# Second projection: pairs of column tiles by seven products in place of eight for half of k

## The chip, the core and the metric

The program runs on one core of one Trainium2 chip. The metric is the device time of one execution in microseconds (us); the time before is 2892.36 us, the median of 3 runs (2892.21 to 2892.92).

The engines are named as in the profile: PE is the matrix engine (PEld its weight loads), DVE, ACT and POOL are the vector, scalar and GpSimd engines, and SP issues the DMAs. Each engine executes its own instructions in the order in which they stand; a semaphore wait holds everything behind it on that engine.

## What is computed

Two blocks of a network run over 512 tokens of width 2048. The first is a gated delta rule with cross attention and an output projection. The second, which the change touches, is this (cut to what matters):

```python
u = rmsnorm(h, norm_w[l])
proj = jnp.einsum('bsd,dc->bsc', u, w_in[l])          # 2048 -> 8200 columns
(ml_q, ml_k, ml_v, ml_o, ml_z, ml_i, ml_f,
 hg_q, hg_f, hg_i, hg_g) = jnp.split(proj, split_points, axis=-1)
...
h_a = mlstm_chunkwise(q_a, k_a, v_a, i_pre, f_pre)     # 4 heads
h_a = rmsnorm(h_a, ml_norm_w[l].reshape(ML_HEADS, ML_DV)).reshape(Bn, S, ML_WIDTH)
y_a = jax.nn.sigmoid(ml_o) * h_a * jax.nn.silu(ml_z)
...
h_b = hgrn2_chunkwise(q_b, k_b, logf_b, i_b)           # 8 heads
h_b = rmsnorm(h_b, hg_norm_w[l].reshape(HG_HEADS, HG_DV)).reshape(Bn, S, HG_WIDTH)
y_b = h_b * jax.nn.silu(hg_g)
h = h + jnp.einsum('bsc,cd->bsd', jnp.concatenate([y_a, y_b], axis=-1), w_out[l])
e = jnp.einsum('bsr,rd->bsd', p[l], w_pe[l])
gate = jax.nn.sigmoid(jnp.einsum('bsd,de->bse', rmsnorm(h, pe_norm_w[l]), w_pg[l]))
h = h + gate * e
```

The einsum called proj is the second projection. All arithmetic is to hold the accuracy of float32.

## The kernel before

**Tiles.** Activations lie transposed, 128 features by 512 tokens a tile. A projection is cut into jobs, one for each 128 output columns (class `Job`): the job's PSUM tile `acc` collects 16 k-tiles of 128. Each float32 operand is split into a high part of type float32r and the rest (`hi`, `lo` of a weight, `x2h`, `x2l` of an activation), and each k-tile costs three matmuls of 512 columns: hi by high, hi by rest, lo by high (`_unit`, L364). The second projection is 65 jobs: one narrow one of 64 columns with two matmuls a k-tile, and 64 full ones.

**Weights.** They come in pieces of four k-tiles, 128 x 512 float32, 256 KB: a DMA into a ring `raw` of RAW = 6 buffers, then ACT copies the piece to `hi`, then DVE subtracts (`lo` = `raw` - `hi`), into rings of SPL = 5 buffers (`_pump`, L315). PE may thus find up to five pieces ready.

**Order.** The program is written by a planner, `Driver.run` (L397): it keeps an estimated clock of each engine, runs whatever task is ready by these clocks, and fills PE with the next matmuls of the job list in between. What it writes is a fixed order on each engine. A task's data are SBUF tiles from a pool of NSLOT = 75 slots of 128 x 512 (`slot`, L225); a task that finds none waits. PSUM has eight banks, of which up to `maxacc` hold accumulators of jobs.

**The second projection.** The activations `x2h`, `x2l` (32 slots) are made by `x2_task` (L1312) while the first block's output projection ends. The list J2 (L1913) goes: the narrow gate job, then for each mLSTM head k, q and two v tiles, then for each HGRN2 head f, q and i, then the gates o, z and g. When a job ends, `scaled` (L1335) multiplies its PSUM tile by the norm on DVE (tile `pr`), and the head's own tasks go on from there: `ml_task` (L1420) and `hg_task` (L1592) are chains of small matmuls with DVE and ACT steps between, which the planner sets between the projection's matmuls. Each chain leaves normalized tiles in slots (`f_hs`), the gates multiply them, `split_task` (L1239) splits the product, and the second output projection (`w_out2`) uses it. The jobs of `w_pe` (tile `p_h`, two k-tiles each) come after that one. POOL does little here: a mask on `rowb` in each mLSTM head and a 128 x 4 copy `hcd` in each HGRN2 head.

The names in the rows below: `acc` a job's accumulator, `pg` the level products of an HGRN2 head, `z` their operands, `u` its state, `oh` its output, `tr` a transpose, `ss` a sum over partitions by a matmul with ones whose operand is split into `qh`, `ql`, `Cs` the state of an mLSTM head.

Of the kernel before, what the change touches and what calls it, by code (L numbers as in the profile page):

```python
# [18 lines left out]
T = 512  # L19
# [4 lines left out]
RAW, SPL = 6, 5  # L24
NSLOT = 75
LV, LP = 0.3, 0.3
AHEAD = 1.5
# [37 lines left out]
class Job:  # L65

    def __init__(self, w, x, evac, n=T, prio=5.0, begin=None, c0=0):
        self.w, self.x, self.evac, self.n, self.prio, self.begin = w, x, evac, n, prio, begin
        self.cols = slice(c0, c0 + n)
        self.kt = w.shape[1]  # L70
        self.narrow = w.shape[2] < 128
        self.ps = None
        self.drop = False

# [8 lines left out]
class Driver:  # L83
# [5 lines left out]
    def __init__(self, tc, wp, psp, sp):  # L89
# [8 lines left out]
        self.spl_end = []  # L98
# [6 lines left out]
        self.nslot = 0  # L105
        self.table = None
# [195 lines left out]
    def add(self, *jobs):  # L302

        pcs = {j: [] for j in jobs}
        for c0 in range(0, max(j.kt for j in jobs), KC):
            for j in jobs:
                if c0 >= j.kt:
                    continue
                n = min(KC, j.kt - c0)
                p = len(self.pieces)  # L310
                self.pieces.append((j, c0, n))
                for k in range(c0, c0 + n):
                    self.units.append((j, k, p, k == c0 + n - 1, j is jobs[-1]))

    def _pump(self):  # L315
        while self.i_dma < len(self.pieces):
            r = self.i_dma - RAW
            if r >= 0 and (r >= self.i_spl or self.spl_end[r][1] > self.clk["pe"]):
                break
            j, c0, n = self.pieces[self.i_dma]  # L320
            raw = self.wp.tile([128, KC, 128], F32, tag="raw", bufs=RAW, name="raw")
            self.nc.sync.dma_start(out=raw[:, :n, :j.w.shape[2]], in_=j.w[:, c0:c0 + n])
            self.pieces[self.i_dma] = (j, c0, n, raw, self.land(n * 128 * j.w.shape[2]))
# [3 lines left out]
        while self.i_hi < self.i_dma and self.i_hi < self.i_mm + SPL:  # L327
            j, c0, n, raw, tau = self.pieces[self.i_hi]
            if tau > self.clk["pe"] and self.i_hi > self.i_mm:
                break  # L330
            hi = self.wp.tile([128, KC, 128], F32R, tag="hi", bufs=SPL, name="hi")
            self.tau = tau
            m = j.w.shape[2]
            self.act(hi[:, :n, :m], raw[:, :n, :m], AF.Copy)
            self.pieces[self.i_hi] = (j, c0, n, raw, hi, self.tau)
            self.i_hi += 1
        while self.i_spl < self.i_hi:
            j, c0, n, raw, hi, tau = self.pieces[self.i_spl]
            if tau > max(self.clk["pe"], self.clk["dve"]) and self.i_spl > self.i_mm:
                break  # L340
            self.tau = tau
            if j.narrow:
                lo = None
                self.tt(hi[:, :n, 64:], raw[:, :n, :64], hi[:, :n, :64], SUB)
            else:
                lo = self.wp.tile([128, KC, 128], F32R, tag="lo", bufs=SPL, name="lo")
                self.tt(lo[:, :n], raw[:, :n], hi[:, :n], SUB)
            self.pieces[self.i_spl] = (j, c0, n, hi, lo, self.tau)
            self.spl_end.append((self.i_spl, self.tau))
            self.i_spl += 1  # L350

    def _unit_tau(self):

        j, k, p, _, _ = self.units[self.i_unit]
        if p >= self.i_spl or not j.x.f[k].done:
            return None
        t = max(self.pieces[p][5], j.x.f[k].tau)
# [5 lines left out]

    def _unit(self):  # L364
        j, k, p, last_of_piece, last_job = self.units[self.i_unit]
        self.i_unit += 1
        _, c0, _, hi, lo, _ = self.pieces[p]
# [1721 lines left out]
```

## Time and profile before

| | |
|---|---|
| median of 3 runs | 2892.36 us (2892.21 to 2892.92) |
| the profiled execution | 2891.97 us |
| its span, first to last instruction | 2890.2 us |
| PE busy | 2847.4 us, 99% of the span, 15032 matmuls |
| DVE busy | 1716.1 us, 59% |
| ACT busy | 1389.9 us, 48% |
| POOL busy | 98.0 us, 3% |
| chain that ended last | PE 34% of the span, DVE 1% |
| granted TensorE clock | 0.996 of full speed |

Busy is the union of an engine's instructions. A matmul's recorded duration is longer than its pitch, since matmuls overlap in the array; the pitch, from one start to the next, is what PE spends on it. The second projection runs from 1674.7 us, its first matmul, to about 2505 us, where the matmuls of `w_out2` take over. Its stretch is one row of the table of windows below.

### The profile page before, as it was taken

Reading aid. Unit: us, or ns where it says so; the run is one execution under the profiler, and the core shown is the slowest. Engines: PE = TensorE matmul, PEld = TensorE weight load, DVE = VectorE, ACT = ScalarE, POOL = GpSimd, SP = SyncE. Lnnn points to the kernel's source line nnn. Section 1 sums busy time; section 2 is a strip of 40 time slices with the busy share of each in tenths; the row PEclk is TensorE's granted clock in tenths of the full one; section 3 lists DMA queues with packets and bytes.
Section 4 is the critical chain, followed back from the end, with each engine's and each line's share of the span. In section 5 each row is a group of like instructions: output and inputs, shape, how many; then the busy total and the mean of one; then the engine's idle time right before and its main releaser. Section 6 shows DMA issues by size and latency. Waiting matters only on the chain. (4 is left out here: it accounts for less than half of the span.)

```text
span 2890.2 us, 41231 instructions
## 1 busy us (share of the span) xinstructions
PE 2847.4 (99%) x15032; PEld 2380.3 (82%) x15032; DVE 1716.1 (59%) x3323; ACT 1389.9 (48%) x2664; POOL 98.0 (3%) x198
## 2 busy tenths in 40 slices
PE   8999999999999999999999999999999999999998
PEld 7877888888888888888888878888888888888887
DVE  6746687778788777645333364556556565444446
ACT  6544545555555555444222344445555565333444
POOL 2000100000000000000000000000000000000001
PEclk9999999999999999999999999999999999999999
DMA  7422323233232322354433433322222222333334
GB/s 238 149 81 95 119 88 99 96 99 101 74 104 95 96 95 95 103 179 124 130 119 119 145 111 108 95 76 84 81 77 81 86 82 91 121 121 111 92 97 150
DMA packets 179020, 311.05 MB, mean 108 GB/s; under 512 B 25344, under 2 KB 32128, under 8 KB 178816
## 3 DMA queue, kind: packets, MB, share of 16 engines
q1 hardware_dynamic: 178816, 308.41, 33.7%
q8 instruction: 118, 1.93, 0.3%
q14 instruction: 86, 0.70, 0.1%
HBM read 292.34 MB, written 15.99 MB: 107 GB/s over the span
## 5 line engine op out<-in xcount | busy, mean ns | idle before, releaser
L155 DVE TENSOR_TENSOR lo<-raw,hi 128x512 fp32r<-128x512 f32 (+1 forms) x956 | 644.1, 686 | 615.7 <-ACT hi L141 602.4
L141 ACT ACTIVATE hi<-raw 128x512 fp32r<-128x512 f32 (+1 forms) x964 | 590.6, 621 | 822.0 <-PE acc L208 688.1
L208 PE MATMUL acc<-xh,hi 128*128 128x512 f32 x1424 | 581.8, 409 | 0.6 <-DVE vb L155 0.6
L208 PE MATMUL acc<-xl,hi 128*128 128x512 f32 x1424 | 555.4, 390 | 0.0
L208 PE MATMUL acc<-xh,lo 128*128 128x512 f32 x1408 | 550.9, 391 | 1.1 <-DVE lo L155 1.1
L208 PE MATMUL acc<-x2h,hi 128*128 128x512 f32 x1040 | 415.4, 399 | 0.0
L208 PE MATMUL acc<-x2l,hi 128*128 128x512 f32 x1040 | 405.3, 390 | 0.0
L208 PE MATMUL acc<-x2h,lo 128*128 128x512 f32 x1024 | 399.7, 390 | 0.0
L208 PEld LDWEIGHTS acc<-xh,lo 128*128 128x128 f32 x1408 | 264.3, 188 | 59.7 <-DVE lo L155 1.9
L208 PEld LDWEIGHTS acc<-xh,hi 128*128 128x128 f32 x1424 | 267.9, 188 | 53.0 <-issue 1.7
L208 PEld LDWEIGHTS acc<-xl,hi 128*128 128x128 f32 x1424 | 268.2, 188 | 51.1 <-issue 1.7
L208 PE MATMUL acc<-ph,hi 128*128 128x512 f32 x768 | 298.8, 389 | 0.0
L208 PE MATMUL acc<-pl,hi 128*128 128x512 f32 x768 | 298.8, 389 | 0.0
L208 PE MATMUL acc<-ph,lo 128*128 128x512 f32 x768 | 298.8, 389 | 0.0
L208 PEld LDWEIGHTS acc<-x2h,hi 128*128 128x128 f32 x1040 | 195.6, 188 | 37.3
L208 PEld LDWEIGHTS acc<-x2l,hi 128*128 128x128 f32 x1040 | 195.8, 188 | 37.0
L208 PEld LDWEIGHTS acc<-x2h,lo 128*128 128x128 f32 x1024 | 192.2, 188 | 41.2
L208 PEld LDWEIGHTS acc<-pl,hi 128*128 128x128 f32 x768 | 144.1, 188 | 30.2
L208 PEld LDWEIGHTS acc<-ph,hi 128*128 128x128 f32 x768 | 144.1, 188 | 29.9
L208 PEld LDWEIGHTS acc<-ph,lo 128*128 128x128 f32 x768 | 144.1, 188 | 29.7
L160 DVE SCALAR_TENSOR_TENSOR cv<-acc,c_dn_conv,cv 128x511 f32<-128x511 f32 x144 | 107.4, 747 | 28.1 <-ACT cv L141 24.4
L155 DVE TENSOR_TENSOR Xb<-Xb,Nb 128x16 f32<-128x16 f32 (+30 forms) x372 | 113.9, 306 | 8.9
(324 smaller groups left out, 3676.6 us busy)
## 6 DMA issues: line engine op xcount, KB each, us to landing
raw<-w_qkv SPq DMA_DIRECT2D x192, 256.0 KB, 3.2
raw<-w_out SPq DMA_DIRECT2D x192, 256.0 KB, 2.9
raw<-w_z SPq DMA_DIRECT2D x128, 256.0 KB, 3.1
raw<-w_pg SPq DMA_DIRECT2D x76, 256.0 KB, 3.2
gR<-dgc SPq DMA_DIRECT2D x48, 256.0 KB, 4.1
raw<-w_k SPq DMA_DIRECT2D x32, 256.0 KB, 5.2
raw<-w_v SPq DMA_DIRECT2D x32, 256.0 KB, 3.5
raw<-w_xq SPq DMA_DIRECT2D x32, 256.0 KB, 3.1
```

The lines of the kernel that those rows point to most:

```text
L141: self.nc.scalar.activation(out=out, in_=in_, func=func, **kw)
L155: self._v(eng, 0.07 + n / 960, 0.43 + n / 590).tensor_tensor(out=out, in0=a, in1=b, op=op)
L160: self._v(None, 0.13 + free_size(out) / 960, 0).scalar_tensor_tensor(out=out, in0=a, scalar=s, in1=b, op0=op0, op1=op1)
L208: self.nc.tensor.matmul(out, lhsT=lhsT, rhs=rhs, start=start, stop=stop, is_transpose=True if tr else None)
```

## The change

For 29 pairs of jobs (58 of the 64 full ones), the first 8 of the 16 k-tiles are computed in another way. Call B11 and B12 the four first k-tiles of the pair's two column tiles, B21 and B22 the next four, and cut the 512 tokens into halves a and b. Eight products of one block of weights with one half of the tokens become seven, of sums and differences (the Winograd form of Strassen's scheme); each is 4 k-tiles by three matmuls of 256 columns. The other 8 k-tiles stay as they were. The narrow job, four first full jobs and two last ones stay single.

Around it:

- Four differences of weights a pair (`wt`, and one in place in `raw`) are made on POOL, and the four products that use them get their hi and lo parts from POOL too (`tp`, a cast and a subtraction, ring of TB = 3). The other pieces still go by ACT and DVE: 7 a pair in place of 8.
- Sums and differences of activations (`s2h`, `s2l`, 16 slots) are made once, on POOL, and split on ACT and DVE (`x2_sums`).
- Two products collect in two extra PSUM tiles a pair; ACT copies them out (`z0`, `z1`), DVE combines them by four additions of 256 columns, and `scaled` has an addition more for each job.
- With 57 of 73 slots held by activations, sums and weights, the heads' results are written to DRAM (`hgs`) and read back when a gate needs them; the jobs of HGRN2 heads and gates alternate.
- RAW is 8 in place of 6, NSLOT 73 in place of 75; six of the `w_pe` jobs are set ahead of `w_out2`.

```diff
-RAW, SPL = 6, 5
-NSLOT = 75
+RAW, SPL = 8, 5
+NSLOT = 73
+TB = 3
...
+    def add_pair(self, pr):
...
+        u = [(j, c) for c in range(2 * KC, j0.kt, KC) for j in (j0, j1)]
+        usual(*u[0])
+        b11, b12 = load(j0, 0), load(j1, 0)
+        b12.made = False
+        usual(*u[1])
+        b22, b21 = load(j1, KC), load(j0, KC)
+        diff(t1, b12, b11)
+        for q, l in ((0, b11), (5, t1)):
+            product(q, l)
+        diff(t2, b22, t1)
+        diff(b12, b22, b12)
+        for v in u[2:-1]:
+            usual(*v)
+        for q, l in ((3, b22), (6, t2), (7, b12)):
+            product(q, l)
+        diff(t4, b21, t2)
+        usual(*u[-1])
+        for q, l in ((2, b21), (4, t4)):
+            product(q, l)
...
+    def _top(self, op, pe):
...
+            if self.i_tp >= self.i_tm + TB:
+                return False
...
+            self.cp(op.hi, l.raw, eng=pool)
+            self.tt(op.lo, l.raw, op.hi, SUB, eng=pool)
...
+        self.tt(dst.raw, x.raw, y.raw, SUB, eng=pool)
...
+    def _products(self, u):
...
+        return {0: (pr.x.f[k], a, "p", a), 2: (pr.x.f[k + KC], a, 0, a), 3: (pr.comb[k][1], b, 1, a),
+                4: (pr.x.f[k + KC], b, 0, b), 5: (pr.comb[k][0], a, "q", a), 6: (pr.comb[k][0], b, "p", b),
+                7: (pr.comb[k][1], a, "q", b)}[q]
...
+        for n, (w, x) in enumerate(((pc.hi, xh), (pc.hi, xl), (pc.lo, xh))):
+            self.tau = 0.0
+            self.mm(ps[:, oc], w[:, k], x[:, c], start=first and n == 0,
+                    stop=end and n == 2 and q not in (2, 3))
...
+    def _sums(self, pr):
...
+        self.act(z0, pr.acc["p"], AF.Copy)
+        self.act(z1, pr.acc["q"], AF.Copy)
+        self.free_bank(2)
+        yield
+        for o, x, y in ((z0[:, b], z0[:, a], z0[:, b]), (z1[:, a], z1[:, a], z0[:, b]),
+                        (z0[:, b], z0[:, b], z1[:, b]), (z1[:, b], z1[:, b], z1[:, a])):
+            self.tt(o, x, y, ADD)
...
+    def x2_sums():
...
+                tt(t, hi, lo, ADD, eng=pool)
...
+            for o, x, y, op in ((s[:, a], u[:, b], v[:, b], ADD), (s[:, b], s[:, a], u[:, a], SUB),
+                                (t[:, a], u[:, a], u[:, b], SUB), (t[:, b], v[:, a], s[:, b], SUB)):
+                tt(o, x, y, op, eng=pool)
...
     def scaled(job):
...
+        t = yield from need(job.z)
+        yield
+        tt(t, t, job.ps, ADD)
         d.acc_done()
+        tt(t, t, r, MUL)
         return t
...
-        give(f_hs[2 * MLH + h], r)
+        if h >= HGH - 2:
+            give(f_hs[2 * MLH + h], r)
+            return
+        yield
+        d.dma(hgs_[2 * MLH + h], r)
+        free(r)
+        give(f_hm[2 * MLH + h])
...
+    seq = mls + hgs[:2]
+    hgs = hgs[2:]
+    for i in range(max(len(hgs), len(gts))):
+        seq += hgs[i:i + 1] + gts[i:i + 1]
+    seq += [tuple(gl[i:i + 2]) for i in range(0, HGH - 2, 2)]
+    for i, (j0, j1) in enumerate(seq):
+        d.add_pair(Pair(j0, j1, X2, f_s2, drop=(i == len(seq) - 1)))
```

What stands on PE in a job of the projection before, the first of four k-tiles with a transpose of a head between:

```order
L208 MATMUL acc_17355<-x2h_13754,hi_17264 128x512
L208 MATMUL acc_17355<-x2l_13755,hi_17264 128x512
L208 MATMUL acc_17355<-x2h_13754,lo_17266 128x512
L208 MATMUL tr_17365<-ident_87,mcv_17030 128x128 x4
L208 MATMUL acc_17355<-x2h_13912,hi_17264 128x512
L208 MATMUL acc_17355<-x2l_13913,hi_17264 128x512
```

And now on PE in the first pair, where product 0 ends and product 5 begins:

```order
L249 MATMUL acc_16631<-x2h_15787,hi_16516 128x256
L249 MATMUL acc_16631<-x2l_15788,hi_16516 128x256
L249 MATMUL acc_16631<-x2h_15787,lo_16518 128x256
L249 MATMUL acc_16652<-s2h_15846,tp_16375 128x256
L249 MATMUL acc_16652<-s2l_15847,tp_16375 128x256
L249 MATMUL acc_16652<-s2h_15846,tp_16376 128x256
```

Over the program 1392 matmuls of 512 columns are gone from PE and 2436 of 256 columns have come; the weights of product 5 are POOL's `tp`.

On POOL, all that stood from the last head of the first block to the end before:

```order
L180 MEMSET XT 128x512 x2
L180 MEMSET XA 128x256
L185 AFFINE_SELECT rowb<-rowb 128x512 x4
L175 COPY hcd<-z 128x4 x8
L155 TENSOR_TENSOR out<-h1r,gt 128x256 x10
```

And now on POOL one pair of the 29 (`wt` and `raw` differences of weights, `tp` their parts):

```order
L196 TENSOR_TENSOR wt_16373<-raw_18492,raw_18421 128x512
L216 CAST tp_16422<-wt_16373 128x512
L196 TENSOR_TENSOR tp_16423<-wt_16373,tp_16422 128x512
L196 TENSOR_TENSOR wt_16402<-raw_18509,wt_16373 128x512
L196 TENSOR_TENSOR raw_18492<-raw_18509,raw_18492 128x512
L216 CAST tp_16375<-wt_16402 128x512
L196 TENSOR_TENSOR tp_16376<-wt_16402,tp_16375 128x512
L216 CAST tp_16418<-raw_18492 128x512
L196 TENSOR_TENSOR tp_16419<-raw_18492,tp_16418 128x512
L196 TENSOR_TENSOR wt_16460<-raw_18589,wt_16402 128x512
L216 CAST tp_16422<-wt_16460 128x512
L196 TENSOR_TENSOR tp_16423<-wt_16460,tp_16422 128x512
```

Eight two-input subtractions and four casts a pair are new on POOL; `rowb` and `hcd` now stand between them.

On DVE, around the end of a job in an HGRN2 head before:

```order
L155 TENSOR_TENSOR lo_19247<-raw_19092,hi_19245 128x512
L155 TENSOR_TENSOR pr_19253<-acc_19127,ssum_13686 128x512
L191 SCALAR_TENSOR_TENSOR b_19255<-resetb_105,b_19255 128x512
L169 TENSOR_SCALAR pr_19253<-pr_19253,oml_13503 128x512
L1661 COPY_PREDICATED at_19025<-lmask_13493,pg_19261 128x512
```

And now on DVE, from the second job of a pair to the first addition of the next pair's `z0`:

```order
L196 TENSOR_TENSOR z1_18435<-z1_18435,acc_18232 128x512
L196 TENSOR_TENSOR z1_18435<-z1_18435,ssum_13691 128x512
L196 TENSOR_TENSOR lo_18519<-raw_18290,hi_18517 128x512
L196 TENSOR_TENSOR lo_18536<-raw_18286,hi_18534 128x512
L196 TENSOR_TENSOR lo_18553<-raw_18403,hi_18551 128x512
L196 TENSOR_TENSOR at_18574<-z0_18434,z1_18435 128x512
L196 TENSOR_TENSOR ql_18577<-at_18574,qh_18576 128x512
L196 TENSOR_TENSOR lo_18597<-raw_18494,hi_18595 128x512
L196 TENSOR_TENSOR lo_18615<-raw_18421,hi_18613 128x512
L196 TENSOR_TENSOR at_18574<-ss_18633,ident_87 128x512
L196 TENSOR_TENSOR kd_18637<-kd_18637,z0_18434 128x512
L196 TENSOR_TENSOR z0_18663<-z0_18663 128x256
```

A job's one multiplication `pr` has become an addition and a multiplication, and a pair has four additions of 256 columns more, in the same queue as the head's own steps (`at`, `ql`, `kd`).

## Rows read from the trace of the kernel before

**Rows 1.** Window: length; busy (count) of PE, PEld, DVE, ACT, POOL; clock; DMA
```profile
1674.70:2505.00 830.30, 826.62 (x4109) 694.37 (x4108) 471.55 (x802) 417.22 (x710) 4.46 (x12) 1.00 0.28 89
```
**Rows 2.** Groups of PE, 1674.7 to 2505: busy us, mean ns; idle before us
```profile
L208 PE MATMUL acc<-x2h,lo 128*128 128x512 f32 x1024 | 399.7, 390 | 0.0
```
**Rows 3.** Waits of PE in the same stretch: us in total, times, longest
```profile
PE tr L208 <- DVE pr L155: 3.4, 3, 2.4
```
**Rows 4.** Timeline of PE, second projection: start us, us; nine pitches apart
```profile
2166.66 0.39 PE L208 MATMUL acc<-x2h,lo 128*128 128x512 f32 x1
...
2168.70 0.39 PE L208 MATMUL acc<-x2h,lo 128*128 128x512 f32 x1
```
**Rows 5.** Timeline of PE, last jobs, 256 columns: 32 pitches apart
```profile
2842.10 0.28 PE L208 MATMUL acc<-x3l,hi 128*128 128x256 f32 x1
...
2845.94 0.28 PE L208 MATMUL acc<-x3h,hi 128*128 128x256 f32 x1
```
**Rows 6.** Groups of DVE, 1674.7 to 2505
```profile
L155 DVE TENSOR_TENSOR lo<-raw,hi 128x512 fp32r<-128x512 f32 x259 | 174.6, 688 | 138.3 <-ACT hi L141 132.8 <-PE acc L208 2.6
L155 DVE TENSOR_TENSOR pr<-acc,ssum 128x512 f32<-128x512 f32 x65 | 44.4, 684 | 11.6 <-PE acc L208 11.6
L155 DVE TENSOR_TENSOR z<-z,pr 128x256 f32<-128x256 f32 x112 | 42.7, 422 | 32.2 <-ACT z L141 32.2
```
**Rows 7.** Groups of ACT, the same stretch: a weight copy, a copy from PSUM
```profile
L141 ACT ACTIVATE hi<-raw 128x512 fp32r<-128x512 f32 x259 | 159.1, 625 | 203.7 <-PE acc L208 169.7 <-issue 25.6 <-DVE mp L180 2.1
L141 ACT ACTIVATE mv<-tr 128x512 f32<-128x512 f32 x8 | 4.8, 596 | 5.9 <-PE tr L208 5.9
```
**Rows 8.** Groups of POOL, whole span
```profile
L155 POOL TENSOR_TENSOR xsum<-xsum,xsq 128x512 f32<-128x512 f32 x15 | 20.8, 1389 | 40.1 <-ACT xsq L141 39.4
L175 POOL COPY xsum<-xsq 128x512 f32<-128x512 f32 x1 | 0.6, 611 | 12.5 <-ACT xsq L141 12.5
```
**Rows 9.** Timeline, POOL and DVE together, 41 to 45 us
```profile
41.55 2.99 POOL L155 TENSOR_TENSOR xsum<-xsum,xsq 128x512 f32<-128x512 f32 x2 [11.30 <-ACT xsq L141]
41.97 1.43 DVE L155 TENSOR_TENSOR lo<-raw,hi 128x512 fp32r<-128x512 f32 x1 [0.27 <-ACT hi L141]
```
**Rows 10.** Timeline, POOL and DVE together at the program's end; `out` of 256 columns
```profile
2879.62 4.41 POOL L155 TENSOR_TENSOR out<-h1r,gt 128x256 f32<-128x256 f32 x5 [11.83 <-ACT gt L141]
2879.57 5.07 DVE L155 TENSOR_TENSOR out<-h1r,gt 128x256 f32<-128x256 f32 x7 [0.47 <-ACT gt L141]
```
**Rows 11.** Tile `out`: duration min/median/max ns on each engine
```profile
L155 DVE TENSOR_TENSOR out<-h1r,gt x16: 411/418/944, 2863.3 to 2884.6; 128x256 f32<-128x256 f32 x16
L155 POOL TENSOR_TENSOR out<-h1r,gt x10: 733/900/1186, 2863.4 to 2883.1; 128x256 f32<-128x256 f32 x10
```
**Rows 12.** Timeline of one HGRN2 head's end and the next one's start
```profile
2158.30 0.34 DVE L160 SCALAR_TENSOR_TENSOR u<-u,hcd,pst 128x128 f32<-128x128 f32 x1
...
2158.73 0.46 PE L208 MATMUL oh<-z,u 128*128 128x128 f32 x2
...
2160.52 0.69 DVE L155 TENSOR_TENSOR ql<-sq,qh 128x512 fp32r<-128x512 f32 x1 [1.88 <-ACT qh L141]
...
2162.04 0.40 PE L208 MATMUL ss<-ql,ones_r 128*128 128x512 f32 x1
...
2162.57 0.69 DVE L155 TENSOR_TENSOR ql<-at,qh 128x512 fp32r<-128x512 f32 x1 [0.76 <-ACT qh L141]
...
2164.59 0.40 PE L208 MATMUL ss<-ql,ones_r 128*128 128x512 f32 x1
```
**Rows 13.** Two more links of the chains, groups of 1674.7 to 2505
```profile
L208 PE MATMUL tr<-ident,pr 128*128 128x128 f32 x64 | 9.8, 276 | 3.7 <-DVE pr L155 3.4
L160 DVE SCALAR_TENSOR_TENSOR Cs<-Cs,wsb,pst 128x384 f32<-128x384 f32 x8 | 4.9, 614 | 12.1 <-PE pst L208 12.1
```
**Rows 14.** When the activations are made: tile `x2h`
```profile
L141 ACT ACTIVATE x2h<-h,c_norm_w x14: 708/708/722, 1359.7 to 1672.5; 128x512 fp32r<-128x512 f32 x14
```
**Rows 15.** DMA issues, 1674.7 to 2505: count, KB each, median us to landing
```profile
raw<-w_mlv SPq DMA_DIRECT2D x32, 256.0 KB, 3.1
```

More of the change, by code (lines that the diff above doesn't have):

```diff
@@ L73, in __init__ @@
         self.drop = False
+        self.z, self.fin, self.stop = None, True, False
+        self.ks = range(self.kt)
+class Pair:
+    def __init__(self, j0, j1, x, comb, drop=False):
+        self.j0, self.j1, self.x, self.comb, self.drop = j0, j1, x, comb, drop
+        for j in (j0, j1):
+            j.z, j.fin = Fut(), False
+        j1.stop = True
+        self.acc = {}
+class PUnit:
+    def __init__(self, pair, q, k, p):
+        self.pair, self.q, self.k, self.p = pair, q, k, p
+class Load:
+    def __init__(self, w, c0, n):
+        self.w, self.c0, self.n = w, c0, n
+        self.raw, self.tau, self.uses, self.end = None, 0.0, 0, None
+        self.made, self.old = w is not None, None
+class Piece:
+    def __init__(self, src, narrow=False, own=True):
+        self.src, self.narrow, self.own, self.ready = src, narrow, own, False
+        self.hi = self.lo = None
+        self.tau = 0.0
+        src.uses += 1
 class Parts:
@@ L105, in __init__ @@
         self.nslot = 0
+        self.pairs = 0
         self.table = None
@@ L302, in add @@
     def add(self, *jobs):
-        pcs = {j: [] for j in jobs}
         for c0 in range(0, max(j.kt for j in jobs), KC):
             for j in jobs:
-                if c0 >= j.kt:
+                if c0 >= j.kt or c0 not in j.ks:
                     continue
                 n = min(KC, j.kt - c0)
-                p = len(self.pieces)
-                self.pieces.append((j, c0, n))
+                self.loads.append(Load(j.w, c0, n))
+                p = Piece(self.loads[-1], j.narrow)
+                self.pieces.append(p)
@@ L312, in add, with load, usual, diff @@
                 for k in range(c0, c0 + n):
                     self.units.append((j, k, p, k == c0 + n - 1, j is jobs[-1]))
+    def add_pair(self, pr):
+        j0, j1 = pr.j0, pr.j1
+        self.pairs += 1
+        for j in (j0, j1):
+            j.ks = range(2 * KC, j.kt)
+        ld = {}
+        def load(j, c):
+            ld[j, c] = Load(j.w, c, KC)
+            self.loads.append(ld[j, c])
+            return ld[j, c]
+        def usual(j, c):
+            p = Piece(load(j, c))
+            self.pieces.append(p)
+            for k in range(c, c + KC):
+                self.units.append((j, k, p, k == c + KC - 1, False))
+        def diff(dst, x, y):
+            self.tops.append((dst, x, y))
+            x.uses += 1
+            y.uses += 1
+            parts[dst] = Piece(dst, own=False)
+        def product(q, l):
+            p = parts.get(l)
+            if p is None:
+                p = Piece(l)
+                self.pieces.append(p)
+            else:
+                self.tops.append(p)
+            for k in range(KC):
+                self.units.append(PUnit(pr, q, k, p))
+        parts = {}
+        t1, t2, t4 = ts = [Load(None, 0, KC) for _ in range(3)]
+        for i, t in enumerate(ts):
+            t.old, self.sums[i] = self.sums[i], t
+        u = [(j, c) for c in range(2 * KC, j0.kt, KC) for j in (j0, j1)]
[17 more added lines that the diff above has]
+            product(q, l)
@@ L337, in _pump @@
[L337 to L350, printed above, removed]
@@ L1938, in build @@
     d.spawn(h1_loader(), 8)
     jo = [Job(A["w_out2"][i], Y2, evac_o2(i), begin=begin_of(f_o2[i])) for i in range(KT)]
-    jo0 = jo[0].begin
-    def begin_o2():
-        jo0()
-        give(f_pb)
-    jo[0].begin = begin_o2
+    je = [Job(A["w_pe"][i], PP, evac_e(i)) for i in range(KT)]
+    for i in range(2, 2 + NPE):
+        d.add(je[i])
+    d.spawn(after(f_pb, p_task(), d), 39)
+    gl[-2].begin = begin_of(f_pb)
+    jo[0].begin = begin_of(f_o2[0])
     d.add(jo[0], jo[1])
@@ L1953, in build @@
         d.spawn(x3_task(w), 9 + 0.1 * w)
-    d.spawn(p_task(), 39)
-    je = [Job(A["w_pe"][i], PP, evac_e(i)) for i in range(KT)]
     jg = [Job(A["w_pg"][i], X3, evac_g(i)) for i in range(KT)]
@@ L1960, in build @@
     for i in range(2, KT - NSP):
-        d.add(je[i])
+        if i >= 2 + NPE:
+            d.add(je[i])
         d.add(jg[i])
```

318 lines of the change are left out of this document (256 added, 62 removed).

## The prediction

> **What bounds the kernel now.** I read the windows first, for the stretch that the change touches. The second projection lasts 830.3 us and PE is busy in 826.6 of them, at full clock, while DVE is busy in 471.6, ACT in 417.2 and POOL in 4.5 [rows 1]. A busy PE could still be a waiting one, so the groups and the waits come next: the weights' own matmuls never stood idle for a piece [rows 2], and all waits of PE here are 3.4 us [rows 3]. So the stretch is as long as PE's matmuls, and what a change gives is what it takes off PE, unless it makes PE wait. The recorded 0.39 us of a matmul overlaps with the next; the price is the pitch. 512 columns: nine pitches are 2168.70 - 2166.66 = 2.04 us, 0.2267 us each [rows 4]. 256 columns with the same 128 x 128 weights: 32 pitches are 3.84 us, 0.1200 us each [rows 5]. Half the columns cost 53%, not 50%, and that eats part of what seven in eight promises.
>
> **PE, the gain.** For a pair, the first half of k was 2 jobs x 8 k-tiles x 3 = 48 matmuls: 48 x 0.2267 = 10.88 us. It becomes 7 products x 4 k-tiles x 3 = 84 of 256 columns: 84 x 0.1200 = 10.08 us. That is 0.80 us a pair and 23.2 us for 29 pairs. With the other half of k (10.88) a pair is then 20.96 us of PE, and the stretch would be 830.3 - 23.2 = 807 us. PE's other work is the same; the six jobs of `w_pe` that are moved are 36 matmuls, 8.2 us, and cost the same in either place.
>
> [...]
>
> **POOL, all new.** A pair puts 8 two-input subtractions and 4 casts there. At 1.39 and 0.61 us [rows 8] that is 8 x 1.39 + 4 x 0.61 = 13.6 us, or 393 us for 29 pairs, 49% of 807. No row has a cast to float32r on POOL; it lies between the copy and the two-input form, so a pair costs at most 12 x 1.39 = 16.7 us, 60%. I take the copy's 0.61, since a cast has one input too. Either way POOL fits. Its pieces are written ahead: by the ring of three, work on product 4 may start when PE has ended product 5, and 2.72 + 3 x 1.44 + 2.72 + 1.44 = 11.2 us of PE lie between. `rowb` now waits for its DMA, and `hcd` for ACT, with `tp` pieces queued behind; those 11 us cover one such wait of a few us. If that cover were gone, PE would wait for product 5, 6, 7 or 4.
>
> **DVE and ACT.** DVE loses one `lo` (0.69), gains four additions of 256 columns at 0.42 and one more full operation for each of the two jobs at 0.68 [rows 6]: -0.69 + 1.69 + 1.37 = 2.37 us a pair, 69 us in all, so 540 us, 67% of 807. ACT gains two copies from PSUM at 0.60 and loses a `hi` of 0.63 [rows 7]: 0.57 us a pair, 17 us, to 54%. In amount both stay hidden.
>
> **Edits that I cost at nothing.** The sums of activations take POOL 4 x (2 x 1.39 + 4 x 0.73) = 23 us [rows 8, 11] once the first eight `x2h` exist; the activations are made by 1672.5 [rows 14], and the narrow job and four single jobs (4.67 x 10.88 = 51 us) run before the first pair. Without that cover it is 23 us at most. The heads' results make 22 writes and 22 reads of 256 KB on SP's queue; a load lands in about 3 us [rows 15] and is asked for when its pair begins, 21 us before the gate. Two more weight buffers, two slots fewer and the order of the first block that moves with them: no PE work changes; bounded by the waits of this stretch, 3 us either way, taken as zero.
>
> **Where part of the gain goes: DVE and POOL get in each other's way.** The trace shows it at two places. A `lo` that began while POOL worked took 1.43 us in place of 0.69 [rows 6, 9], 0.74 late, as if it had stood until POOL's operation ended. At the end of the program seven DVE and five POOL operations of 256 columns run side by side: DVE's take 5.07 us instead of 7 x 0.41 = 2.9, 0.44 late for each operation of POOL [rows 10, 11]. Now POOL works half of the time.
>
> Lateness of a `lo` hurts little: ACT waits 169.7 us in total for PE to free a weight buffer [rows 7], that is, weights are prepared as far ahead as the ring allows. The heads' chains are tight. A state `u` ends at 2158.64 and its matmul starts at 2158.73, 0.09 us later; a `ql` at 2161.21 and its sum at 2162.04, 0.83; the next at 2163.26 and 2164.59, 1.33 [rows 12]. PE is in order and the order is fixed, so a link later than its margin stops PE, and what feeds DVE from PE shifts with it: such stalls add up. I count two `u` and two `ql` for each of 8 HGRN2 heads, 16 transposes that wait for a `pr` and 8 states `Cs` [rows 13]: 32 + 16 + 8 = 56 links. A link's operation is between 0 and 0.74 us late, 0.37 in the middle when it meets POOL, and it meets it 49% of the time: 0.18. The margins swallow part, and the queue ahead of it, late too, adds; I take 0.2 us a link, 11 us. Ends: 0 and 56 x 0.74 = 41 us.
>
> **Sum.** -23.2 + 11.2 = -12 us. The profiled execution took 2891.97 us (span 2890.2, 1.8 around it), 0.4 under the median, so I count from the median: 2892.4 - 12 = 2880 us. With 0.2% (5.8 us, about what a measurement of this kernel can tell from no change) as a border, this case runs from 2871 to 2886.
>
> **Rivals.**
> *All hidden.* Margins and idle time of DVE swallow the lateness; the stretch is 807 us: 2869. For it: DVE waits 138 us before `lo` alone [rows 6], room to be late in. Against: the margin of 0.09 us.
> *The links eat the gain.* At 0.31 to 0.5 us a link, 17 to 28 us, the time is within 0.2% of before, about 2891. For it: in a head the late operations follow each other.
> *DVE becomes the bound, slower.* If every operation of POOL meets a busy DVE, a pair adds 8 x 0.74 + 4 x 0.33 (the copy by its length) = 7.2 us to DVE, 210 us in all: 540 + 210 = 750 of 807, 93%. DVE also has to wait for ACT and PE inside the chains: 182 us before the three groups of [rows 6]. From 57 us of such waiting that can't be used, it sets the pace. If 100 us stay, the stretch is 850 us, 20 more than before: 2912. If all stay, 932 us. Place: the pairs between HGRN2 heads, where DVE has most to do. Against: POOL also meets waits of DVE, where it costs nothing.
> [...]
> *Slots run out.* 57 of 73 are held, so evacuations wait and PSUM banks stay taken. Priced by PE's longest wait for one, 2.4 us [rows 3], once a pair: 70 us, less 23: 2939.
> That the change would not take the work off PE is no case: the order has 1392 matmuls of 512 columns fewer and 2436 of 256 more.
>
> **Chances.** Forecast 0.40, all hidden 0.14, links eat the gain 0.18, DVE the bound 0.24, slots 0.04. Faster 0.54, same 0.18, slower 0.28. The range: down to 2866, the full gain and the 3 us of the first block; up to 2918, which holds the DVE case at 2912 and leaves out its tail and the slots.
>
> **What would show it.** In the profile after: the pitch of the `s2h` matmuls 0.120 us; POOL busy near 390 to 480 us more, its subtractions near 1.4 to 1.7 us; DVE's `lo` above 0.69 in the mean; waits of PE for `u`, `ql`, `pr` of some 10 us, and none for `tp`. If PE waits for `tp`, the cover of 11 us was wrong. If DVE's busy time passes 700 us in the stretch, the third rival holds. If matmuls of 256 columns between 512s take more than 0.120, the first term is wrong.

## The result and the profile after: slower by 3.6%

The changed kernel takes 2994.21 us in the median (2992.79 to 2996.41, 4 runs) where the kernel before takes 2892.28. The ratio is 1.0356, 95% interval 1.0342 to 1.0369. The forecast was 2880, the range 2866 to 2918. The profiled execution has a span of 2992.7 us.

The page of the changed kernel, part 1 (busy us, share, instructions), the slices of DVE and POOL, and the shares of the chain that ended last:

```profile
PE 2865.4 (96%) x16076; PEld 2436.0 (81%) x16076; DVE 1996.5 (67%) x3476; ACT 1395.4 (47%) x2699; POOL 578.9 (19%) x570
...
DVE  6736777788777778453333775688888888743546
...
POOL 2000100000000000000000443555465555100001
...
PE 26%; DVE 10%; issue 3%; ACT 2%; POOL 0%; DMA 0%; DVEq 0%; ACTq 0%; POOLq 0%; SPq 0%
```

The chain was 34% PE and 1% DVE; now a tenth of the span hangs on DVE. Of the twelve slices in which POOL now has 3 to 6 tenths, DVE stands at 8 tenths in eight.

The windows answer [rows 1]: the stretch from the second projection's first matmul to the first one of `w_out2`, with the six moved jobs of `w_pe` (8.2 us) in it; length, busy (count) of PE, PEld, DVE, ACT, POOL, granted clock, DMA share, GB/s:

```profile
1673.70:2612.30 938.60, 850.80 (x5175) 755.00 (x5174) 739.96 (x951) 424.19 (x745) 458.27 (x363) 0.96 0.31 92
```

Cut in the same way, the stretch before is 1674.7 to 2502.0, 827.3 us, so 111.3 us were added here. 7.8 us of it are given back behind it, since the moved jobs are gone there, and 1.0 us came ahead of it: 111.3 - 7.8 - 1.0 = 102.5, the whole difference of the spans. Without the 8.2 us the stretch took 930 us; on this cut the forecast's first term said 827.3 - 23.2 = 804, and 815 with the links. PE stands idle for 87.8 us and DVE is busy in 740 us, 79%.

Waits of PE in this stretch (us in total, times, longest); before there were 3.4 us [rows 3]:

```profile
PE pg L249 <- DVE z L196: 20.3, 14, 3.7
PE oh L249 <- DVE u L201: 16.2, 10, 4.0
PE tr L249 <- DVE pr L196: 11.1, 2, 10.7
PE tr L249 <- DVE mcv L210: 9.9, 3, 4.1
PE ss L249 <- ACT qh L182: 7.5, 7, 3.6
PE ss L249 <- DVE ql L196: 7.0, 8, 3.3
```

None is for `tp`, for a slot or for a DMA; the list goes on with 15.4 us in four more lines, all of them DVE's. All but the 4.7 us of the `acc` lines are waits in the heads' chains, but only some are of the kinds that the prediction had counted: `u`, `pr` and `ql` make 34.3 us in 20 waits, `Cs` none. The other 53.1 us of the list's 87.4 are at links that it had not counted, the level products `pg` with their operand `z` first.

Groups of DVE in the stretch (busy us, mean ns; idle before), to be held against [rows 6], where `lo` took 688 ns and a `z` of 256 columns 422 (the second group here has eight of 512 columns among its 178):

```profile
L196 DVE TENSOR_TENSOR lo<-raw,hi 128x512 fp32r<-128x512 f32 (+1 forms) x234 | 240.1, 1053 | 27.4 <-ACT hi L182 26.1
L196 DVE TENSOR_TENSOR z<-z,z 128x256 f32<-128x256 f32 (+1 forms) x178 | 124.1, 723 | 38.5 <-ACT z L182 31.8 <-POOL hcd L216 3.7
L196 DVE TENSOR_TENSOR z<-z,ssum 128x512 f32<-128x512 f32 x58 | 47.7, 822 | 2.0
L196 DVE TENSOR_TENSOR z<-z,acc 128x512 f32<-128x512 f32 x58 | 39.3, 678 | 0.0
```

The last two rows have the same size and differ in one operand: `ssum` lies in SBUF, `acc` in PSUM. Of the two, only the operation with both inputs in SBUF is late: 822 ns in the mean against 692 where POOL's operations are narrow (the first run below), the one with `acc` 678 against 680. How it comes about is seen in the timeline; POOL first, then DVE:

```profile
2203.20 1.74 POOL L196 TENSOR_TENSOR wt<-raw,wt 128x512 f32<-128x512 f32 x1
2204.91 1.74 POOL L196 TENSOR_TENSOR raw<-raw 128x512 f32<-128x512 f32 x1
2206.59 1.07 POOL L216 CAST tp<-wt 128x512 fp32r<-128x512 f32 x1
```

```profile
2203.72 3.48 DVE L196 TENSOR_TENSOR lo<-raw,hi 128x512 fp32r<-128x512 f32 x2
2207.12 0.68 DVE L196 TENSOR_TENSOR at<-ss,ident 128x512 f32<-128x512 f32 x1
2207.72 0.68 DVE L196 TENSOR_TENSOR kd<-kd,z 128x512 f32<-128x512 f32 x1
```

Two `lo` take 3.48 us in place of 1.38 (twice the 688 ns of [rows 6]), one POOL operation each in between. Behind them stand `at` and `kd`, and PE waits for `kd`:

```profile
2206.53 0.28 PE L249 MATMUL acc<-x2h,lo 128*128 128x256 f32 x1
2208.45 0.65 PE L249 MATMUL tr<-ident,kd 128*128 128x128 f32 x4 [1.65 <-DVE kd L196]
```

Last, what comes behind a wait. Windows of the same kernel around a wait for `mcv` of 4.1 us that ends at 1822.0, and PE's timeline after it:

```profile
1808.00:1817.70 9.70, 9.70 (x71) 9.14 (x69) 1.75 (x3) 1.26 (x2) 7.16 (x8) 1.00 0.50 127
1817.70:1822.00 4.30, 0.17 (x2) 0.01 (x1) 0.43 (x1) 3.78 (x8) 0.47 (x1) 1.00 0.00 0
1822.70:1826.10 3.40, 3.40 (x13) 2.83 (x12) 3.32 (x4) 1.24 (x3) 3.07 (x3) 0.51 0.02 5
1826.20:1833.00 6.80, 6.80 (x43) 6.04 (x43) 5.78 (x10) 1.45 (x2) 0.75 (x1) 1.00 0.55 154
```

```profile
1817.59 0.28 PE L249 MATMUL acc<-x2h,tp 128*128 128x256 f32 x1
1822.02 0.63 PE L249 MATMUL tr<-ident,mcv 128*128 128x128 f32 x4 [4.14 <-DVE mcv L210]
...
1822.89 0.63 PE L249 MATMUL acc<-x2h,hi 128*128 128x512 f32 x1
1823.32 0.63 PE L249 MATMUL acc<-x2l,hi 128*128 128x512 f32 x1
```

Behind the wait the granted clock is at 0.51 from 1822.7 to 1826.1 us, and the pitch of 512 columns is 0.43 us (1823.32 - 1822.89) in place of 0.227 [rows 4]; from 1826.2 the clock is at 1.00. So this wait is paid for twice, in idle time and by the clock.

### The profile page after: what moved, and what is told of

Its sections match the earlier page's. It is cut to its first block, busy times and chain, and to the rows that moved or that the text cites. A ratio compares the mean times of both kernels' runs of the same rounds, so it can differ in the third digit from the quotient of the medians.

```text
span 2992.7 us, 44256 instructions
## 1 busy us (share of the span) xinstructions
PE 2865.4 (96%) x16076; PEld 2436.0 (81%) x16076; DVE 1996.5 (67%) x3476; ACT 1395.4 (47%) x2699; POOL 578.9 (19%) x570
## 5 line engine op out<-in xcount | busy, mean ns | idle before, releaser
L196 DVE TENSOR_TENSOR lo<-raw,hi 128x512 fp32r<-128x512 f32 (+1 forms) x927 | 709.7, 782 | 493.4 <-ACT hi L182 475.3
L182 ACT ACTIVATE hi<-raw 128x512 fp32r<-128x512 f32 (+1 forms) x935 | 567.9, 620 | 699.5 <-PE acc L249 580.2
L249 PE MATMUL acc<-x2h,hi 128*128 128x512 f32 (+1 forms) x808 | 306.4, 379 | 0.0
L249 PE MATMUL acc<-x2l,hi 128*128 128x512 f32 (+1 forms) x808 | 297.5, 368 | 0.0
L249 PE MATMUL acc<-x2h,lo 128*128 128x512 f32 (+1 forms) x792 | 290.7, 367 | 2.8 <-DVE lo L196 2.8
L249 PEld LDWEIGHTS acc<-x2h,lo 128*128 128x128 f32 x792 | 153.6, 194 | 27.6 <-DVE lo L196 3.0
L249 PEld LDWEIGHTS acc<-x2h,hi 128*128 128x128 f32 x808 | 158.0, 196 | 21.6
L249 PEld LDWEIGHTS acc<-x2l,hi 128*128 128x128 f32 x808 | 157.7, 195 | 20.8
L182 ACT ACTIVATE z<-z 128x256 f32<-128x256 f32 (+1 forms) x142 | 60.3, 463 | 204.2 <-DVE z L196 183.3
L196 DVE TENSOR_TENSOR z<-z,z 128x256 f32<-128x256 f32 (+1 forms) x178 | 124.1, 723 | 38.5 <-ACT z L182 31.8
```

Source lines behind the costliest of these rows:

```text
L182: self.nc.scalar.activation(out=out, in_=in_, func=func, **kw)
L196: self._v(eng, 0.07 + n / 960, 0.43 + n / 590).tensor_tensor(out=out, in0=a, in1=b, op=op)
L249: self.nc.tensor.matmul(out, lhsT=lhsT, rhs=rhs, start=start, stop=stop, is_transpose=True if tr else None)
```

## Experiments

Two theories were open at first. **A**: DVE and POOL hold each other up, DVE gets late, PE waits and its clock falls. **B**: DVE has too much to do and the heads' new order is too tight, whatever POOL does.

### POOL's operations made short

```diff
-            self.cp(op.hi, l.raw, eng=pool)
-            self.tt(op.lo, l.raw, op.hi, SUB, eng=pool)
+            m = slice(0, 128 if self.i_tp < TB else 2)
+            self.cp(op.hi, l.raw, eng=pool, m=m)
+            self.tt(op.lo, l.raw, op.hi, SUB, eng=pool, m=m)
```

(The differences likewise; the planner goes on charging the whole operation, so the order is the same.)

> The changed kernel with the same instructions in the same order, but POOL's twelve operations of a pair work on 8 of 512 columns (whole only where a buffer is used for the first time), so the weights of four products are wrong and POOL's operations are short. Theory A (DVE and POOL hold each other up, and PE then waits and its clock falls): DVE's lo goes back from 1.06 to about 0.7 us, the waits of PE above 0.6 us fall from 92 us to under 25 us, and the time is 2866 to 2895 us. Rival B (DVE has too much to do and the new order of the heads is too tight, whatever POOL does): waits of PE stay at 70 to 90 us and the time at 2970 to 2995 us. Rival C (the matmuls of 256 columns themselves bring the clock down): clock as low as in the changed kernel, 2980 us or more.

Measured: 2878.88 us (2876.78 to 2879.62), ratio 0.9953 (0.9938 to 0.9967). The stretch, `lo` in it, and PE's longest wait:

```profile
1675.80:2497.80 822.00, 809.41 (x5175) 730.13 (x5174) 545.21 (x951) 426.57 (x745) 123.49 (x363) 0.99 0.35 105
```

```profile
L198 DVE TENSOR_TENSOR lo<-raw,hi 128x512 fp32r<-128x512 f32 (+1 forms) x234 | 155.6, 688 | 51.5 <-ACT hi L182 49.3
PE tr L253 <- DVE pr L198: 10.3, 2, 9.9
```

The same 5175 matmuls, 951 DVE and 363 POOL instructions as in the changed kernel, so the two rows can be subtracted. DVE: 740.0 - 545.2 = 195 us, its lateness. PE idle: 87.8 - 12.6 = 75.2 us. PE busy: 850.8 - 809.4 = 41.4 us, the same matmuls at a lower clock (0.96 against 0.99). 75.2 + 41.4 = 116.6 us is the difference of the two stretches; every microsecond of idleness came with 0.55 us more by the clock. The time, the waits and `lo` are all as theory A had them; rival B, 2970 us or more whatever POOL does, falls. Rival C falls: the 256-column matmuls are all here, and the clock is at 0.99.

Of the 12.6 us that PE still waits, 10 are one wait for `pr` that begins at 1720: the first pair's POOL operations are mostly whole in this run too. By an estimate from these two numbers, without that wait the time would be about 2869, the prediction's "all hidden".

### The new order without the seven products

```diff
-        for j in (j0, j1):
-            j.ks = range(2 * KC, j.kt)
...
+        self.add(j0, j1)
```

> The changed kernel without the seven products: all 29 pairs as eight products, sixteen k-tiles by matmuls of 512 columns, no sums and no POOL work for them; the new order of jobs, eight weight buffers, 73 slots, the writing and reading of the heads' results and the moved w_pe jobs stay. Theory A: the order costs next to nothing, 2885 to 2905 us. Rival B (the order is too tight): of the 125 us of loss a third or more is here already, 2930 us or more.

Measured: 2897.22 us (2894.29 to 2900.97), ratio 1.0019 (1.0009 to 1.0028), within theory A's range. The order, the writing and reading of the heads' results, the two buffers and the moved jobs cost 4.6 us together, which the prediction had set at nothing.

### POOL's work alone, in the kernel before

```diff
+            if extra:
...
+                self.nc.gpsimd.tensor_tensor(out=self.scr, in0=raw, in1=raw, op=SUB)
```

(The second run has `tensor_copy(out=self.scr, in_=raw)` in that place.)

> The kernel before, with one more POOL operation for each weight piece of the 64 full jobs (256 in all, 8 for two jobs): a subtraction of a weight buffer from itself into a scratch tile that nobody reads. No other instruction changes. Theory A (the exclusion of DVE and POOL alone makes PE wait): lo rises above 0.8 us in the mean and the time by 10 to 60 us, 2902 to 2952 us. Rival B (DVE's own added work decides): within 6 us of 2892.

> As the run with 256 added subtractions on POOL, but each is a copy (one input) of the weight buffer to the scratch tile. Theory A with the lock held by any POOL operation that reads SBUF, for its length: a lo that meets one is late by up to about 0.6 us in place of 1.4, the loss is a third to a half of that run's. Rival (only POOL's two-input operations lock DVE out): lo stays at 0.69 us and the time within 6 us of 2892.

Measured: 2911.02 us with subtractions (ratio 1.0066, 1.0049 to 1.0083), 2895.86 with copies (1.0013, 1.0004 to 1.0022). Groups of DVE in the second projection, with subtractions first, with copies second:

```profile
L156 DVE TENSOR_TENSOR lo<-raw,hi 128x512 fp32r<-128x512 f32 x258 | 214.1, 850 | 91.2 <-ACT hi L142 86.7 <-PE acc L209 2.6
L156 DVE TENSOR_TENSOR pr<-acc,ssum 128x512 f32<-128x512 f32 x64 | 43.6, 681 | 6.8 <-PE acc L209 6.8
```

```profile
L156 DVE TENSOR_TENSOR lo<-raw,hi 128x512 fp32r<-128x512 f32 x258 | 189.0, 748 | 119.5 <-ACT hi L142 115.0 <-PE acc L209 2.3
```

DVE's lateness needs nothing of the change: 256 subtractions that nobody reads make DVE 85 us busier (554.3 against 469.3) and the kernel 18 us slower; PE's waits there are at `pr`, `u`, `kd`, `z` and `Cs`, none for a weight piece. The copies make `lo` late as well, by 60 ns in the mean, so the rival is wrong in its mechanism, that only two-input operations of POOL make `lo` late; its time, within 6 us of 2892, is the one that came. They cost 3 us, a sixth of the loss with subtractions, where I had expected a third to a half. And 18 us is far from 116: POOL's work alone, beside a DVE that is busy in 554 of 846 us, is not the whole story.

### The work moved off POOL, or part of it

```diff
-            self.cp(op.hi, l.raw, eng=pool)
-            self.tt(op.lo, l.raw, op.hi, SUB, eng=pool)
+            self.act(op.hi, l.raw, AF.Copy)
+            self.tt(op.lo, l.raw, op.hi, SUB)
...
-        self.tt(dst.raw, x.raw, y.raw, SUB, eng=pool)
+        self.tt(dst.raw, x.raw, y.raw, SUB)
```

(The second run leaves the differences, the last two lines, on POOL and has a ring of two; in the first, a gate's loaded tile also leaves four slots free.)

> The changed kernel with POOL's twelve operations of a pair given to other engines: the eight subtractions to DVE (29 x 8 x 0.69 = 160 us more), the four casts to ACT (29 x 4 x 0.62 = 72 us more); the planner knows both prices, and a gate's loaded tile leaves four slots free. Theory A (what cost the time was DVE made late in ways that the order did not know): DVE is busy in about 550 + 160 = 710 us, nearly as long as in the changed kernel (725), but on time, and PE waits little: 2866 to 2895 us. Rival B (DVE has simply too much to do, whoever causes it): with 710 us the waits of PE are those of the changed kernel, 2950 us or more.

> Between the two: POOL keeps the four differences of a pair (116 in all, about 180 us), the casts go to ACT and the four lo to DVE (80 us more on it); the ring of parts is two in place of three. Theory A: POOL's time in two-input operations falls from 360 us to 180, and with it the lateness of DVE to less than half of 205 us; the time lies between the run without POOL and the changed kernel, 2885 to 2940 us. Rival B (amount of DVE work): as the changed kernel, 2970 us or more.

Measured: 2954.47 us (ratio 1.0214, 1.0197 to 1.0231) and 2963.04 us (1.0245, 1.023 to 1.0261). Theory A as I had put it fails in both. Rival B has the first, 2950 or more, but not the second, 2970 or more. In the first nothing is late: `lo` takes 681 ns. Yet PE is idle for 57 us:

```profile
1675.00:2557.20 882.20, 825.19 (x5119) 739.89 (x5118) 663.10 (x1158) 480.71 (x846) 6.67 (x14) 0.97 0.32 97
```

```profile
PE acc L249 <- ACT hi L182: 24.0, 6, 7.9
PE pg L249 <- DVE z L196: 9.2, 4, 7.3
PE acc L249 <- DVE lo L196: 6.2, 6, 2.5
```

Part of it is a queue of its own: a `tp` cast on ACT waits for DVE's difference (46.2 us in total ahead of these casts), and the `hi` of the next usual piece stands behind it. Of the run's 56.7 us of waits, 33.6 are for `hi`, `lo` and `tp`, the weights; the heads' chains have 20, where the changed kernel has 83. In the second run 40.6 of 68.5 us are for `tp` alone. So these two runs show that the work costs time wherever it stands, but most of their loss is a queue of weights and doesn't speak for DVE in the chains. They raised another reading, F: what counts is how full DVE is, whatever fills it.

### The planner told of the lateness

```diff
+            late = 1.5 if two and self.pairs and hasattr(self, "f_pd") else 1.0
-            self._on("dve", cost, LV)
+            self._on("dve", late * cost, LV)
```

> The changed kernel with POOL's work as it is, but the planner prices every DVE operation without a PSUM operand 1.5 times as high while pairs run, so it sets what PE does for the heads later and other matmuls in between; the ring of parts is two in place of three and a gate's loaded tile leaves four slots free. Theory A1 (PE waits because the fixed order was made for undisturbed durations): the waits of PE above 0.6 us fall from 92 us to 45 or less and the time to 2890 to 2935 us. Rival A2 (DVE is at its limit, with lateness, so no order helps): 2960 us or more.

Measured: 2982.42 us (2980.55 to 2983.9), ratio 1.0311 (1.0296 to 1.0327): 12 us better than the changed kernel and no more, as rival A2 had it. DVE is still busy in 692.6 of the stretch's 886.0 us, PE idle for 61 us, and behind it the rest of the program takes 422 us in place of 380, with some hundred of the stretch's matmuls now in it (5073 are left of 5175): heads that were set later end later. This order, made for durations 1.5 times as long, doesn't bring the loss back; other prices weren't tried.

### DVE relieved, with POOL as it is

```diff
+                        if l in self.short:
+                            p.lo = p.hi
+                            self._v(None, 0.07 + n * 128 / 960, 0)
...
```

> The changed kernel with POOL's work whole, but the 203 lo of the pairs' own weight pieces left out on DVE: those matmuls use hi once more in place of lo, so the low parts of these weights are missing. Every other instruction is there in the same order. DVE loses 203 x 0.69 = 140 us of work and the lateness of these lo, some 80 us. Theory F (what counts is how full DVE is, lateness included): DVE is busy below 65% of the stretch, the waits of PE above 0.6 us fall from 92 us to under 30 and the time to 2868 to 2905 us. Rival L (single links: an operation of a head that meets POOL is late by up to POOL's operation and PE waits for it, however full DVE is): the heads' operations still meet POOL as often, the waits stay above 50 us and the time at 2930 us or more.

Measured: 2905.27 us (2903.12 to 2906.52), ratio 1.0049 (1.0032 to 1.0066). PE is idle for 30 us. The row of the stretch, and a group that is still late:

```profile
1674.00:2520.70 846.70, 816.46 (x5176) 732.85 (x5175) 549.45 (x748) 425.69 (x745) 423.40 (x363) 0.99 0.33 102
```

```profile
L197 DVE TENSOR_TENSOR z<-z,z 128x256 f32<-128x256 f32 (+1 forms) x178 | 133.7, 777 | 43.6 <-ACT z L183 34.6 <-POOL hcd L217 6.0
```

The heads' `z` are as late as in the changed kernel (777 ns against 723), POOL is busy in 423 us, and still 89 of the 115 us between the changed kernel and the run with narrow operations are gone. L, the single links, expected 2930 or more and is wrong; F's upper ends are reached: 2905.27 us lies just above its 2905, the 30 us of waits and DVE's 65% at theirs. The links do cost something by themselves: with the same busy DVE (549 against 545 us) this run has 18 us more of idle PE than the run with narrow operations.

### Pairs at the gates only

```diff
+        if (j0, j1) in whole:
+            d.add(j0)
+            d.add(j1)
+        else:
+            d.add_pair(Pair(j0, j1, X2, f_s2, drop=(i == len(seq) - 1)))
```

> The changed kernel with seven products only for the 11 pairs of gate jobs; the 18 pairs of mLSTM and HGRN2 jobs go by eight products. From the run of the order alone, 2897 us, 11 x 0.80 = 8.8 us are gained, 2888 us. Theory F: DVE has some 465 + 26 + 80 (lateness) = 570 us, as full as in the run with POOL's narrow operations, so 5 to 20 us of it are lost again: 2890 to 2908 us. Rival L: a gate's pair runs beside the HGRN2 heads, so each of their links near it still waits: 2915 us or more.

> As the run with 11 pairs, but the differences and the lo of their sums on DVE and the casts on ACT; POOL does none. Theory F: DVE has 465 + 26 + 61 = 552 us, with nothing late, and PE waits 0 to 15 us more than in the run of the order alone: 2886 to 2902 us, a candidate for a version no slower than before. Rival (the pieces made on ACT and DVE stand ahead of the usual ones in their queues, so PE waits for hi and lo whatever the fill, as in the run without POOL): 11/29 of that run's 80 us or more, 2918 us.

Measured: 2907.15 us (ratio 1.0055, 1.004 to 1.007) and 2900.81 us (1.003, 1.0018 to 1.0041). Both lie in F's ranges, near the upper ends, and neither gets below the kernel before: the 8.8 us of 11 pairs are less than what the order (4.6 us) and the waits (12 and 6 us more of idle PE than in the run of the order alone) take.

### DVE filled without POOL

```diff
+                            for _ in range(1 + self.nmore % 2):
+                                self.extra(l)
...
+        self.nc.vector.tensor_tensor(out=self.scr, in0=l.raw, in1=l.raw, op=SUB)
```

(On top of the run with POOL's narrow operations; the second run leaves out the `1 +`.)

> The run with POOL's narrow operations (2879 us, waits of PE 11.5 us), and on DVE, unknown to the planner, 305 more subtractions of a weight buffer from itself into a scratch tile, behind the lo of the pairs' pieces by turns two and one: 305 x 0.69 = 210 us, as much as the lateness of DVE in the changed kernel (205 us). POOL holds nobody up here. Theory F (DVE's time counts, whatever fills it): DVE is busy in 750 us of the stretch, PE waits 60 to 110 us, 2950 to 3010 us. Rival P (it needs the lock, since only that hits the heads' operations themselves): below 2920 us.

> The same with 102 more subtractions on DVE, one behind every second of these lo: 70 us, DVE busy in about 615 us (74% of the stretch). Theory F with a knee: the loss lies well under a third of that of the run with 305, so 2880 to 2915 us. Rival (loss in proportion to DVE's time): a third of it, 2905 to 2925 us. Rival P: 2876 to 2885 us.

Measured: 2965.37 us (2964.95 to 2965.86) and 2884.44 us (2882.48 to 2885.74), that is 86.5 and 5.6 us above the run without these subtractions. The stretch with 305 of them, with `lo` and two of its waits, and the stretch with 102:

```profile
1673.90:2583.40 909.50, 839.29 (x5176) 744.35 (x5175) 732.23 (x1256) 423.04 (x745) 145.15 (x363) 0.98 0.31 95
L199 DVE TENSOR_TENSOR lo<-raw,hi 128x512 fp32r<-128x512 f32 (+1 forms) x234 | 160.2, 687 | 18.4 <-ACT hi L183 16.0
PE oh L254 <- DVE u L204: 11.7, 9, 2.3
PE ss L254 <- ACT qh L183: 10.5, 10, 3.1
```

```profile
1674.50:2502.20 827.70, 811.28 (x5176) 730.82 (x5176) 605.05 (x1053) 425.27 (x745) 142.16 (x363) 0.99 0.35 104
```

F holds with its knee: a third of the work costs a fifteenth of the loss. The run with 102 lies in rival P's range too; the one with 305 is far above P's 2920. Work whose result nobody waits for, with `lo` at 687 ns and POOL busy in 145 us, gives 86.5 us, where 115 lie between the changed kernel and the run with narrow operations. Its waits are those of the heads' chains; only 0.7 us of them are for a weight piece.

### All runs in one table

| kernel | time | stretch | DVE busy | DVE idle | PE idle |
|---|---|---|---|---|---|
| before | 2892 | 827 | 469 | 358 | 4 |
| order only | 2897 | 841 | 473 | 368 | 6 |
| before + copies on POOL | 2896 | 831 | 498 | 333 | 5 |
| POOL narrow | 2879 | 822 | 545 | 277 | 13 |
| POOL whole, `lo` left out | 2905 | 847 | 549 | 297 | 30 |
| gates, no POOL | 2901 | 841 | 553 | 288 | 12 |
| before + subtractions on POOL | 2911 | 846 | 554 | 292 | 16 |
| gates, POOL | 2907 | 850 | 567 | 283 | 18 |
| POOL narrow + 102 on DVE | 2884 | 828 | 605 | 223 | 16 |
| no POOL | 2954 | 882 | 663 | 219 | 57 |
| differences on POOL | 2963 | 906 | 672 | 234 | 69 |
| planned late | 2982 | 886 | 693 | 193 | 61 |
| POOL narrow + 305 on DVE | 2965 | 910 | 732 | 177 | 70 |
| changed kernel | 2994 | 939 | 740 | 199 | 88 |

The column to read is DVE idle, with what lies behind it. What DVE gives up first is idle time ahead of `lo`, which is made in advance: 138 us before, 52 with POOL narrow, 36 with 102 more on DVE, 27 in the changed kernel, 18 with 305 more. The idle time ahead of all its other groups, above all waits inside the chains of heads and gates for ACT and PE, in which DVE's queue has nothing that it may do, goes down far less: 220, 225, 187, 171 and 159 us in the same order. In these runs the loss grows steeply where DVE's idle time comes below some 220 us: at 223 us (102 more) PE is idle for 16 us, at 177 to 199 us for 61 to 88. The two runs without casts on POOL (219 and 234 us) don't fit this line, since most of their waits are for weights.

## Why the prediction was wrong, point by point

- **PE's gain: right.** The pitch of 256 columns came out as forecast: on the changed kernel's timeline five pitches from 1816.27 to 1816.87 are 0.60 us, 0.120 each. With POOL narrow the stretch is 822.0 - 8.2 = 813.8 us, and 805 when PE's idle time is set back to what it was before (12.6 against 3.7); on this cut the forecast is 827.3 - 23.2 = 804.

```profile
1816.27 0.28 PE L249 MATMUL acc<-x2h,hi 128*128 128x256 f32 x1
...
1816.87 0.40 PE L249 MATMUL acc<-x2h,tp 128*128 128x256 f32 x2
```

- **POOL's load: right, and no bound.** 454 us more in the stretch (458.3 against 4.5), within the 390 to 480 that were to be looked for; no wait of PE for `tp`.

```profile
L196 POOL TENSOR_TENSOR tp<-wt,tp 128x512 fp32r<-128x512 f32 x87 | 129.9, 1493 | 7.0
L216 POOL CAST tp<-wt 128x512 fp32r<-128x512 f32 x87 | 72.0, 828 | 281.1 <-PE acc L249 280.9
```

- **DVE's own work: right.** 540 us were counted; 545 were measured where POOL is narrow. **Its lateness: right as the third rival had it**, 210 us at most, 195 measured. Whether nearly every operation of POOL met a busy DVE, as that rival had supposed, wasn't counted: a DVE operation (`z<-z,ssum`) was late by up to 1.06 us (1753 ns against 693 in the median), more than the 0.74 that it was priced at. The prediction's own sign for that rival, DVE busy for over 700 us in the stretch, came: 740.
- **The likeliest case: wrong, and this is the step that failed.** It took the lateness link by link, 56 x 0.2 us = 11 us, with 41 us as the worst. Measured were 87.8 us of idle PE. Two things were wrong in that term. The count: 53.1 us of the waits are at places outside the kinds that make up the 56. And the price: here a link wasn't late just by the one operation of POOL that it met; it was late by all that its queue had gathered. The run with the `lo` left out shows the difference: the links as late as ever, and 30 us in place of 88. The run with 305 subtractions shows it from the other side.
- **The third rival had the mechanism and a price that was too low.** It let 100 of the 182 us of waits stay, without a row that spoke for 100. It also wrote down what happens if all stay: 932 us, and the stretch took 930. That the two agree is luck. 138 of the 182 us are ahead of `lo`, which is no step of a head's chain (the case "all hidden" had called the same 138 us room to be late in), and of these only 27 stayed. The waits that do hold DVE are spread over its other groups, 220 us before and 171 in the changed kernel, and the prediction had read 44 of them.
- **A term was missing.** The rows before show full clock in the whole stretch [rows 1], and I priced every wait by its length alone. The lower clock (0.96 against 0.99 in the stretch) makes 41 of the 116 us between the changed kernel and POOL narrow. With 305 subtractions it is alike: 57.6 us more of idle PE came with 29.9 us more of busy PE, 0.52 for each.
- **Edits taken as free: 4.6 us**, by the run of the order alone; 3 us were allowed.
- **The sums of activations: hidden, as taken.** On POOL they end by 1678, before the first pair, though the last two `x2h` start at 1674.5 and 1679.3 and not by 1672.5 ([rows 14] has 14 of the 16); the sums need the first eight. What stands out there is the first pair's POOL work: it makes the wait for `pr` at 1720 10 us long, where it is 2.3 us in the run of the order alone, without sums, and 2.2 us in the run without POOL in the pairs, with them.
- **Slots: right as far as seen.** A lack of slots would show in the order that the planner writes and not as a wait; POOL narrow has the same order and the same slots and took 2879 us.
- **Range.** It cut the tail of the third rival at 2918 while its own end stood at 932 us of stretch, some 2994 us of time (2892 + 932 - 830): the measured value, by the luck told above. With 0.24 on that case, the tail should have been inside.

What is not settled: of the 115 us between the changed kernel and the run with POOL narrow, 86.5 come from as much plain work on DVE. The other 29 may be the links' own lateness (18 us of idle PE in the run with the `lo` left out speak for it) or the larger share of DVE idle time (199 against 177 us); no run tells these apart. In the changed kernel and in the run with 305 subtractions the planner doesn't know of the time that fills DVE; how much an order made for it could give back is known for one price alone (12 us). A version that beats both kernels wasn't found: the differences of the weights need either DVE, which has some 70 us to give (102 subtractions, 71 us, cost 5.6), or POOL, which makes DVE late.

## What to carry to other kernels

An engine that works inside chains isn't free until it is 100% busy: here PE stood idle for 88 us with DVE busy in 79% of the stretch. Add to its busy time the waits that it has inside the chains (rows of the kernel before show them as idle time ahead of the chains' groups), leave out idle time ahead of work that is made in advance, and ask whether the sum still fits the stretch. Here such waits were 220 us before and 159 to 171 where DVE was fullest, so the sum is a warning and no exact bound; beyond it each microsecond of idle PE came with half a microsecond more by the clock (0.55 and 0.52 us). Here work put on POOL beside DVE operations with two SBUF inputs counted as DVE's work, too: 335 us more of POOL (458 against 123) made DVE 195 us late.

## What the runs showed of the hardware

The DVE addition that reads PSUM was not late beside POOL, which was busy in half of the stretch (458 of 939 us): 58 of them took 671 to 681 ns. The operation of the same size with both inputs in SBUF was late by up to 1.06 us, and one with an SBUF input and scalars by up to 0.99. Tile answers of the changed kernel (duration min/median/max in ns):

```profile
L196 DVE TENSOR_TENSOR z<-z,acc x58: 671/679/681, 1763.6 to 2587.4; 128x512 f32<-128x512 f32 x58
L196 DVE TENSOR_TENSOR z<-z,ssum x58: 691/693/1753, 1764.3 to 2588.1; 128x512 f32<-128x512 f32 x58
L210 DVE TENSOR_SCALAR z<-z,oml x8: 460/464/1452, 1959.4 to 2507.3; 128x512 f32<-128x512 f32 x8
```

Why the one form was late and the other not, no run shows. The delay was at most 1.06 us for one of these operations; that 29 pairs with such operations cost the kernel 102 us is a matter of the chains behind it.

POOL's subtractions took 1.49 to 1.63 us in the mean here against 1.39 for an addition of the same size before [rows 8]; that DVE makes them longer is likely, but not shown apart from the other operands. One of 8 columns still took 0.27 to 0.40 us in the mean in the run with POOL's narrow operations, so cutting POOL's operations into smaller ones would not be free.
